# A hybrid decoder layer on one core: modulation sums moved to the u and c stages, FFN2's first group taken last, another prologue, narrower rotors

## The chip, the cores and the metric

The kernel runs on one core of a Trainium2 chip. The core has a matrix engine (TensorE, PE in the profile, with its weight loads as PEld), VectorE (DVE), ScalarE (ACT), GpSimd (POOL) and SyncE (SP), which issues nearly all DMA transfers here. Each engine works through its own instructions in program order; semaphores make one wait for another. The metric is the device time of one execution in microseconds, as the median of several. A second kernel differs from the first by the diff further down, and the question is how its time stands to the first one's.

## What is computed

One decoder layer over 1024 tokens of width 1024, all in f32: a half-step SwiGLU feed-forward net (FFN1, inner width 2816), a mixer of a gated convolution and a diagonal state-space model side by side, a second SwiGLU net (FFN2), and a final norm. Each sub-layer's input is RMS-normalised and modulated by a shift and a scale, and its output by a gate; these nine vectors are `silu(cond) @ w_mod + b_mod`.

```python
c_act = silu(cond)
sh1, sc1, g1, sh2, sc2, g2, sh3, sc3, g3 = split(c_act @ w_mod + b_mod, 9)
h = modulate(rms_norm(x, ffn1_norm), sh1, sc1)
x = x + 0.5 * g1 * swiglu(h, ffn1_w_gate, ffn1_w_up, ffn1_w_down)
h = modulate(rms_norm(x, mix_norm), sh2, sc2)
b, c, v, u = split(h @ w_in, 4)                       # 512 columns each
y_conv = b * conv3_causal(c * v)
y_ssm = glu(gelu(s5(u)))                              # 32 groups x 64 complex states
x = x + g2 * (concat(rms_norm(y_conv), rms_norm(y_ssm)) @ w_out)
h = modulate(rms_norm(x, ffn2_norm), sh3, sc3)
x = x + 0.5 * g3 * swiglu(h, ffn2_w_gate, ffn2_w_up, ffn2_w_down)
return rms_norm(x, final_norm)
```

## The kernel before

Activations lie transposed: x is eight tiles of 128 channels by two token halves (h = 0 and 1) of 512 columns. Every f32 product is made of three matmuls (`mm3`, L333): weights and activations are each split into a rounded high part and a low part (hi·hi, hi·lo, lo·hi). A weight tile therefore costs ACT one copy and DVE one subtraction (`w<-raw` in the profile), an activation tile the same (`split_act`, L346).

**Weights.** `Weights` (L114) holds the order of all weight arrays (1 MB each, called raw, two buffers) and of the *granules* made of them (1024 columns, split, called w). A granule is made when a slot of the ring comes free (`free`, `pump`), a raw is loaded when an earlier one has given its last granule (`ahead`).

**Clock.** The program is written out by Python. `mm3` ticks a `Clock` (L59) once for its three matmuls. Work put on it with `after(ticks, fn)` is emitted that many ticks later; every `period` ticks one step of a *side* generator is emitted. So the clock sets where, in each engine's order, side work stands among the matmuls. In the prologue the order is the written one (`InOrder.strict`).

**Stages.** PE goes through p (FFN1's group 0, the only one whose products start while the inputs land), fa1 to fa10 (the other ten groups of 256 inner columns; from fa4 on a seven-product scheme, `seven`, L575, replaces eight block products), fad and fald (the down product: eight groups in seven-product form, `down7`, and groups 0, 9 and 10 plainly), u, c and v, the states, b, glu (gl), w_out (wo), then FFN2: fb0, fb1 to fb10, fbd, and fb10d as the last plain part. Results of a group that its down product needs later are stored to DRAM (`keep`, L482; tensors keptN) and fetched back (`fetch`).

**Prologue** (L735 to L824). SP issues the load of tile 0's modulation weights (mw), x, the first raw, mw 1, mw 2, the second raw, then the other mw. `mods_of(k)` (L762) makes tile k's scale and shift: two sums of 128x1024 on DVE and two small operations. Then come the sums of squares, `roots` (an inverse square root in some 13 small DVE operations) and, tile by tile, the normalised and modulated activations. For tiles 0 and 1 there are two weights, w[0] and w[1], for the first two products; the other two are made after tile 1, and their products for tiles 0 to 2 come with tile 2's.

**Modulation sums.** The other seven vectors are 56 sums of one 128x1024 weight tile (wm) with the activated condition (cact): `mod_vector` (L452), one DVE instruction and a read each, in the order of `later`: G1, SC2, SH2, G2, SC3, SH3, G3, eight sums each. `mod_tile` sums one and issues the load of a next one on SP, so loads run a few sums ahead. G1 comes among fa's products; SC2, SH2, G2 in the second half of the down product (`side2`, L1132, period 8, L1209); SC3, SH3, G3 while glu and w_out run (L1414 onwards, period 8, then none, then 3), with cact fetched back from DRAM (cact_d). In the down product the wm tiles lie in the 20 buffers of activations (movA).

**State-space set-up** (`ssm_base`, `ssm_batch` L1031): side work among fa1 to fa10. For eight batches of four groups it makes matrices for the later state recursion and stores them. `rotors(i, op)` (L1069) makes the cosine (co) and sine (si) rotation tables from a base table (16 entries, rt) and a step table (8 entries, rs): two products and a sum, of 128x512 each. The two halves of the 128 partitions carry the same angles, for the sine with opposite signs.

**u, c, v and the states.** `u` is made for token half 0 (four weights at once), then half 1, weight by weight; after each, `across` (L1268) stores a tile to u_d in eight small transfers. Behind the last, `state_loads` loads a batch back in another layout (ub). `states(b)` (L1337) and `outputs(b)` (L1362) are put on the clock at 20 + 16b and 42 + 16b ticks: px (PE) from ub, X (ACT), an exchange of halves by DMA (swx), three DVE operations, a scan of four, si and co (DVE), another exchange (swz), co again, then yy (PE) and a gelu. Both exchanges use one buffer (sw). `outputs(b)` also issues the loads of later batches. Between them PE runs c and v, whose products DVE multiplies (cs), and the convolution (ya) runs on DVE.

**glu and w_out.** The two branch norms nA and nB are on the clock: sums (nBast), roots on DVE, a wide copy (nBarb), a spread by PE (nBabc).

**FFN2.** `group0` (L1503) makes group 0's inner activations, fb_0a and fb_1a; `down2` (L700) multiplies them by their down weights within fb1, between fb1's first and second granule, 96 matmuls and 16 updates `x<-fb0d,gate,x`. `combos` makes meanwhile the block sums (S1 to S4) that `seven` needs. The last part (L1568 on) takes groups 9 and 10 only: for each of eight output tiles d, token half 0 in 512 columns, half 1 partly in two pieces of 256, twelve matmuls per tile; `after2` (L1548) collects the final norm's squares, and the first sums come 6 ticks after d = 7, the spread another 11 ticks later.

Of the kernel before, what the change touches and what calls it, by code (L numbers as in the profile page):

```python
# [21 lines left out]
P = 128  # L22
# [16 lines left out]
LAST = ((0, NGRP - 2, NGRP - 1), (NGRP - 2, NGRP - 1))  # L39
# [77 lines left out]
class Weights:  # L117
# [7 lines left out]

    def __init__(self, engines, srcs, granules, raw_bufs):
# [9 lines left out]
        self.sums_pool = None  # L136
        self.slots = deque()
# [22 lines left out]
    def combine(self, j):  # L160
# [5 lines left out]
        self.sums[j] = {"t1": r[1], "t2": r[0], "t3": f, "t4": r[0]}  # L166

    def split_done(self, j, c):

        if j in self.combined and c in (0, "t2"):  # L170
# [61 lines left out]
def hymba_layer(ctx: ExitStack, tc, x_d, wm1_d, wmod_d, gu1_d, gs1_d, ds1_d, wl1_d, win_d, wout_d, glu_d, gu2_d, gs2_d, wd2_d, ds2_d, wl2_d, cols_d, cond_d, lam_d, bc_d, out_d):  # L232
# [54 lines left out]
    def stream(gu, gs, wd, ds, wl, m):  # L287


        for g in range(m):  # L290
            plain([gu[2 * g], gu[2 * g + 1]])
        for g in range(m, NGRP):
            j = len(srcs)
            inner = g == 1
            srcs.extend([gs[g - m, 0], wd, gs[g - m, 1]] if inner else [gs[g - m, 0], gs[g - m, 1]])
            seven = [(i, c) for i in (j, j + 1 + inner) for c in Weights.SEVEN]
            seven = [seven[i : i + 2] for i in range(0, 14, 2)]
            if inner:
                granules.extend(seven[:1] + [[(j + 1, 2 * q), (j + 1, 2 * q + 1)] for q in range(2)] + seven[1:])
            else:  # L300
                granules.extend(seven)
# [5 lines left out]
        plain([wl[i] for i in range(wl.shape[0])])  # L307

    stream(gu1_d, gs1_d, None, ds1_d, wl1_d, SEVEN_FROM[0])
    plain([win_d[i] for i in range(8)] + [glu_d] + [wout_d[i] for i in range(4)])  # L310
    stream(gu2_d, gs2_d, wd2_d, ds2_d, wl2_d, SEVEN_FROM[1])
    ws = Weights((V, A, SP, nc.gpsimd), srcs, granules, 2)
    ws.raw_pool = lambda i: rawp
# [162 lines left out]
    def gu_evac(fi, h, pg, pu, a_tiles, name):  # L476
        sg, af = t2k(f"{name}sg"), t2k(f"{name}af")
        A.activation(sg[:], pg[:], AF.Silu)
        V.tensor_tensor(out=af[:], in0=sg[:], in1=pu[:], op=ALU.mult)
        a_tiles[fi, h] = split_act(af[:], name + "a")  # L480

# [37 lines left out]

    def down(h, wd, groups, n, name, after):  # L520

        for d0 in range(0, KT, 4):
            outs = [ps(f"{name}d{d}_{h}") for d in range(d0, d0 + 4)]
            for q, a_tiles in enumerate(groups):
                for fi in range(2):
                    for i, o in enumerate(outs):
                        mm3(o[:], wd[2 * q + d0 // 4], 4 * fi + i, a_tiles[fi, h], q == fi == 0, q == len(groups) - 1 and fi == 1)
            for i, o in enumerate(outs):
                d = d0 + i
                V.scalar_tensor_tensor(out=x[d][h], in0=o[:], scalar=gate[:, n, d : d + 1], in1=x[d][h], op0=ALU.mult, op1=ALU.add)  # L530
                if after is not None:
                    after(d, h)
# [42 lines left out]
    def seven(name, between, place=1, kept=None, then=None):  # L575
# [4 lines left out]
        for side in "gu":  # L580
# [17 lines left out]
            for n, (left, b) in enumerate(SEVEN):  # L598
# [45 lines left out]
                if side == "g" and n == place:  # L644
                    between()
                if side == "u" and then is not None:
                    then(left)
        return a_tiles

# [50 lines left out]
    def down2(a_tiles, n, name, halves=(1, 0)):  # L700
        wd = ws.take(2)
        for dh in range(2):
            for h in halves:
# [957 lines left out]
```

## Time and profile before

| | |
|---|---|
| median of three runs | 1749.49 us (1746.47 to 1751.61) |
| the profiled execution's own time | 1752.1 us |
| its span, first to last instruction | 1750.3 us |
| granted TensorE clock, mean over the span | 0.989 |
| share of the span in the chain that ended last | PE 76%, DVE 14%, DMA 5%, issue 2% |
| HBM traffic over the span | 171 GB/s |
| DVE, weight splits w<-raw | 295.9 us in 358 operations |
| DVE, modulation sums wm | 76.6 us in 56 operations |

In a row of instruction groups stand the source line, engine, operation, output <- inputs by the program's names, then minimum, median and maximum duration in ns, or busy us and mean ns. Nearly all instructions have line 107, since a helper records them; tile names tell the stages apart. A row of a timeline begins with its start in us and the time it covers, and ends with its count and, in brackets, the idle time ahead of it and what ended that. A row of waits ends with total us, times and the longest. A busy PE is not PE at full clock: the granted clock is shown by window.

### The profile page before, as it was taken

To read this page: it belongs to the slowest core of one execution; us is meant where nothing else is said; L and a number is where in the kernel's file an instruction comes from. 1 tells how busy PE (TensorE), PEld (TensorE's weight loads), DVE (VectorE), ACT (ScalarE), POOL (GpSimd) and SP (SyncE) were. 2 spreads that over 40 slices of the span, in tenths; PEclk is the share of its full clock that TensorE was granted. 3 is DMA by queue.
4 is the path that set the end of the run, shared out by engine and by line. 5 is a ranking of instruction groups with operands and counts; after the bars stand their busy time and mean duration, and the time that the engine had idled before them with its cause. 6 is when DMAs were issued, how large, how long until landed. Compare 5 with 4: busy or idle time off the path is not lost.

```text
span 1750.3 us, 20808 instructions
## 1 busy us (share of the span) xinstructions
PE 1677.9 (96%) x7532; PEld 1379.6 (79%) x7532; DVE 1300.6 (74%) x2286; ACT 566.0 (32%) x934; POOL 351.1 (20%) x241
## 2 busy tenths in 40 slices
PE   4999999999999999999999899989999999999996
PEld 3788887878787888887877778778888888888886
DVE  7999999999855687744656977967777666676656
ACT  4223234444322221332113424423343443322221
POOL 0000132222222221100000022023323322333211
PEclk9999999999999999999999999999999999999998
DMA  8245544444597877134654450113444334669312
GB/s 319 85 145 196 207 167 165 182 169 178 196 391 266 326 256 292 56 84 149 210 157 140 144 191 25 48 46 135 157 162 173 147 133 156 239 242 366 115 49 96
DMA packets 101080, 304.54 MB, mean 174 GB/s; under 512 B 19057, under 2 KB 34673, under 8 KB 89842
## 3 DMA queue, kind: packets, MB, share of 16 engines
q1 hardware_dynamic: 100978, 303.22, 48.4%
q8 instruction: 59, 0.97, 0.2%
q14 instruction: 43, 0.35, 0.1%
HBM read 212.47 MB, written 86.51 MB: 171 GB/s over the span
## 4 chain that ended last, share of the span: by engine, by line
PE 76%; DVE 14%; DMA 5%; issue 2%; POOL 1%; ACT 1%; SPq 1%; DVEq 0%; POOLq 0%; ACTq 0%
PE wo L107 4%; PE fald L107 3%; DVE w L107 3%; PE p L107 2%; PE fb10d L107 2%; PE fbd_0B L107 2%; PE fbd_1B L107 2%; PE u L107 2%; DMA swz<-si 2%; PE b L107 1%; DVE x L107 1%; PE c L107 1%; PE fa3u L107 1%; PE fb0g L107 1%; PE fa2g L107 1%
## 5 line engine op out<-in xcount | busy, mean ns | idle before, releaser
L107 ACT CAST w<-raw 128x512 fp32r<-128x512 f32 (+1 forms) x358 | 236.2, 689 | 484.3 <-issue 75.0
L107 DVE TENSOR_TENSOR w<-raw,w 128x512 fp32r<-128x512 f32 (+1 forms) x358 | 295.9, 845 | 107.3 <-ACT w L107 106.5
L164 POOL TENSOR_TENSOR sums<-raw 128x512 f32<-128x512 f32 x50 | 71.4, 1429 | 451.5 <-DMA raw<-in_gs 263.3
L173 POOL TENSOR_TENSOR raw<-sums,raw 128x512 f32<-128x512 f32 x50 | 77.7, 1554 | 371.1 <-DVE w L107 358.9
L175 POOL TENSOR_TENSOR raw<-raw 128x512 f32<-128x512 f32 x50 | 77.5, 1549 | 89.6 <-DVE w L107 73.0
L107 DVE CUSTOM_DVE_ANT_0 wm<-wm,cact 128x1024 f32<-128x1024 f32 x56 | 76.6, 1375 | 16.9 <-DMA wm<-in_wmod 16.9
L165 POOL TENSOR_TENSOR raw<-raw 128x512 f32<-128x512 f32 x50 | 77.3, 1547 | 3.2
L366 POOL TENSOR_TENSOR n3aq<-n3aq,n3aq 128x512 f32<-128x512 f32 x5 | 8.3, 1666 | 281.4 <-DMA wm<-in_wmod 255.7
L107 PE MATMUL p<-h,w 128*128 128x512 f32 x192 | 50.0, 423 | 8.0 <-DVE h L107 5.1
L107 DVE TENSOR_TENSOR w<-sums,w 128x512 fp32r<-128x512 f32 x50 | 52.5, 1063 | 3.6 <-ACT w L107 3.0
L107 PEld LDWEIGHTS p<-h,w 128*128 128x128 f32 x192 | 39.4, 207 | 18.4 <-DVE h L107 6.4
L107 PE MATMUL v<-h,w 128*128 128x512 f32 x192 | 46.9, 395 | 0.0
L107 PE MATMUL c<-h,w 128*128 128x512 f32 x192 | 46.6, 395 | 0.0
L107 PE MATMUL wo<-oa,w 128*128 128x512 f32 x192 | 45.6, 392 | 0.9 <-DVE w L107 0.7
L107 PE MATMUL b<-h,w 128*128 128x512 f32 x192 | 45.6, 394 | 0.0
L107 PE MATMUL wo<-ob,w 128*128 128x512 f32 x192 | 45.5, 392 | 0.0
L107 PE MATMUL u<-h,w 128*128 128x512 f32 x192 | 44.7, 392 | 0.2 <-DVE h L107 0.2
L107 PEld LDWEIGHTS wo<-oa,w 128*128 128x128 f32 x192 | 35.8, 188 | 9.0 <-DVE w L107 1.1
L107 PEld LDWEIGHTS u<-h,w 128*128 128x128 f32 x192 | 35.7, 188 | 8.2 <-DVE h L107 0.6
L107 PEld LDWEIGHTS wo<-ob,w 128*128 128x128 f32 x192 | 35.8, 188 | 7.7 <-DVE ob L107 0.4
L107 PEld LDWEIGHTS b<-h,w 128*128 128x128 f32 x192 | 35.6, 188 | 7.1
L107 PEld LDWEIGHTS c<-h,w 128*128 128x128 f32 x192 | 35.4, 188 | 7.0
(1565 smaller groups left out, 4056.2 us busy)
## 6 DMA issues: line engine op xcount, KB each, us to landing
raw<-in_gs SPq DMA_DIRECT2D x34, 1024.0 KB, 5.5
wm<-in_wmod SPq DMA_DIRECT2D x56, 512.0 KB, 5.3
raw<-in_ds SPq DMA_DIRECT2D x16, 1024.0 KB, 7.2
raw<-in_gu SPq DMA_DIRECT2D x10, 1024.0 KB, 7.0
mw<-in_wm SPq DMA_DIRECT2D x8, 1024.0 KB, 12.8
x<-in_x SPq DMA_DIRECT2D x16, 512.0 KB, 8.0
raw<-in_win SPq DMA_DIRECT2D x8, 1024.0 KB, 5.4
raw<-in_wl SPq DMA_DIRECT2D x5, 1024.0 KB, 6.7
```

Of the source, the lines that this page charges most:

```text
L107: r = getattr(self.engine, name)(*args, **kw)
L164: self.G.tensor_tensor(out=f, in0=r[2], in1=r[1], op=ALU.subtract)
L165: self.G.tensor_tensor(out=r[1], in0=r[1], in1=r[0], op=ALU.subtract)
L173: self.G.tensor_tensor(out=r, in0=s["t3"], in1=r, op=ALU.add)
L175: self.G.tensor_tensor(out=r, in0=self.chunk(j, 3), in1=r, op=ALU.subtract)
L366: nc.gpsimd.tensor_tensor(out=a, in0=a, in1=sq[:, :n], op=ALU.add)
```

## The change

Five edits:

1. *Prologue.* mw 1 is loaded before the first raw, and both raws before mw 2; `mods_of(1)` comes before the roots. Tiles 0 and 1 are normalised and modulated together; the other two weights are made right after, and products of all four weights run for both tiles, then four for each further tile.
2. *Rotors.* Base and step tables are kept in a packed form with two groups on each half of the partitions, so that the three operations are 128x256. Each half's result is stored to both halves in DRAM, for the sine with one negated copy by ACT.
3. *x.* The last x loads of FFN1's down product are issued after its third left operand (A22), not its second.
4. *Modulation sums.* G2 leaves the down product. G2, SC3, SH3 and G3 (32 sums) start with u's second token half, at period 3; what is left is emitted before b. glu and w_out have none; cact stays in SBUF.
5. *FFN2's group 0.* Its activations are kept in DRAM like group 9's; `down2` is gone; the last part of the down product has groups 0, 9 and 10. fb1 is made by a new function, `seven_early`, with its own order of the seven products, gate and up side together; a fourth ring slot is opened for the last part.

```diff
-LAST = ((0, NGRP - 2, NGRP - 1), (NGRP - 2, NGRP - 1))
+LAST = ((0, NGRP - 2, NGRP - 1), (0, NGRP - 2, NGRP - 1))
...
+    EARLY = (0, 3, "t4", "t1", "t2", "t3", 2)
...
+            if g == 1:
+                two = j, j + 1
+                granules.extend([(j, c), (j + 1, c)] for c in Weights.EARLY)
             else:
-                granules.extend(seven)
+                seven = [(i, c) for i in (j, j + 1) for c in Weights.SEVEN]
+                granules.extend(seven[i : i + 2] for i in range(0, 14, 2))
...
+    EARLY = (("A11", "A"), ("A12", "A"), ("A22", "E"), ("S1", "C"), ("S2", "B"), ("S3", "D"), ("S4", "C"))
+
+    def seven_early(name, kept):
...
+        for left, b in EARLY:
+            (w,) = ws.take()
+            for q, side in enumerate("gu"):
...
+                for k in range(4):
+                    while len(blocks[left]) <= k:
+                        clock.step()
+                    mm3(bank[b][:], w, 4 * q + k, blocks[left][k], opens and k == 0, k == 3, more=not opens)
...
+            ws.free()
...
     mod_load(0)
     load_x(range(2))
-    ws.load(1)
-    for k in range(1, KT):
+    mod_load(1)
+    ws.load(2)
+    for k in range(2, KT):
         mod_load(k)
-        if k == 2:
-            ws.load(2)
...
+    mods_of(1)
     y = roots(st, 8, D, "p")
...
+    for k, h in ((0, 0), (1, 0), (0, 1)):
+        scaled(k, h)
+    shifted(0)
+    scaled(1, 1)
+    shifted(1)
+    for k in range(2):
         for h in range(2):
...
+            part(h, k, (0, 1))
+    ws.open(ringp, 1)
+    ws.open(ring1, 1)
+    w4 += ws.take(2)
+    for k in range(2):
         for h in range(2):
...
+            part(h, k, (2, 3))
+    for k in range(2, KT):
+        mods_of(k)
+        for h in range(2):
+            scaled(k, h)
+        shifted(k)
         if k < KT - 1:
-            for h in range(2):
-                part(h, k, (0, 1))
-            for j in range(0 if k == 2 else k, k + 1) if k > 1 else ():
+            for outs in ((0, 1), (2, 3)):
                 for h in range(2):
-                    part(h, j, (2, 3))
+                    part(h, k, outs)
...
-    cact_d = scratch.tile([P, 1024], F32, name="cact_d")
-    SP.dma_start(cact_d[:], cact[:])
...
-            return a[:, :512].rearrange("p (g m i) -> p g m i", g=GB, m=8)
+            return a[:, :256].rearrange("p (g m i) -> p g m i", g=2, m=8)
...
-            V.tensor_tensor(out=r[:, :512], in0=r[:, :512], in1=t[:, :512], op=op)
-            SP.dma_start((co_d, si_d)[i][b], r[:, :512])
+            V.tensor_tensor(out=r[:, :256], in0=r[:, :256], in1=t[:, :256], op=op)
+            if i:
+                A.activation(r[:, 256:512], r[:, :256], AF.Identity, scale=-1.0)
+            for q, half in enumerate(halves):
+                to = slice(256 * q, 256 * q + 256)
+                if i == 0:
+                    SP.dma_start(
+                        co_d[b].rearrange("(d p) f -> p d f", d=2)[:, :, to], r[half, :256].unsqueeze(1).to_broadcast([64, 2, 256])
+                    )
+                else:
+                    SP.dma_start(si_d[b][half, to], r[half, :256])
+                    SP.dma_start(si_d[b][halves[1 - q], to], r[half, 256:512])
...
-    down7("fad0", lefts[0], 0, lambda left: fetch_chunk(1, left), lambda left: load_x(range(2), (1, 3)) if left == "A12" else None)
+    down7("fad0", lefts[0], 0, lambda left: fetch_chunk(1, left), lambda left: load_x(range(2), (1, 3)) if left == "A22" else None)
     clock.period = 8
-    clock.side.append(side2(mod_mov, (SC2, SH2, G2)))
+    clock.side.append(side2(mod_mov, (SC2, SH2)))
...
             ready(act2, h, KT)
+            clock.period = 3
+            clock.side.append(side2(mod_mov, (G2, SC3, SH3, G3)))
             for i in range(4):
...
+    while clock.side:
+        clock.step()
     wb = ws.take(4)
...
-    clock.period = 8
-    clock.side.append(side2(lambda name: wmp.tile([P, 1024], F32, tag="wm", name=name, bufs=2)[:], (SC3, SH3, G3)))
...
-    seven("fb1", lambda: down2(a_prev, 2, "fb0", (0, 1)), 0, kept[1])
+    seven_early("fb1", kept[1])
...
+    ws.sums_pool = None
+    first_open.close()
+    sums_open.close()
+    ring1 = ctx.enter_context(tc.tile_pool(name="ring1c", bufs=1))
+    ws.open(ring1, 1)
...
+    def last_part(dh, h, tok, tiles, free=False):
+        outs = {d: ps(f"fb10d{d}_{h}_{tok.start}") for d in tiles}
+        for q, (w, a) in enumerate(zip(wd, (*a_last, a_prev))):
+            for fi in range(2):
+                for d, o in outs.items():
+                    mm3(o[:, tok], w, 4 * fi + d % 4, a[fi, h], q == fi == 0, q == 2 and fi == 1, tok)
...
     for dh in range(2):
-        wd = ws.take(2)
+        wd = ws.take(3)
         for h in range(2):
             for tok in PIECES[h] if dh else WHOLE:
...
+                ds = range(4 * dh, 4 * dh + 4)
+                if h and not dh:
+                    last_part(dh, h, tok, ds, True)
+                else:
+                    for d in ds:
+                        last_part(dh, h, tok, [d])
+    ws.free(3)
```

More of the change, by code (lines that the diff above doesn't have):

```diff
@@ L136, in __init__ @@
         self.sums_pool = None
+        self.early = ()
         self.slots = deque()
@@ L518, in proj @@
         return o
[L520 to L532, printed above, removed]
     blocks = {}
@@ L573, in hymba_layer, with seven @@
     SECOND = (("A11", "A"), ("S2", "B"), ("A12", "A"), ("S3", "B"), ("S1", "C"), ("A22", "B"), ("S4", "C"))
-    def seven(name, between, place=1, kept=None, then=None):
+    def seven(name, kept=None, then=None):
         a_tiles, gate_, taken = {}, {}, []
@@ L1016, in ssm_base @@
                 n *= 2
-        for i in range(2):
-            A.copy(baset[i][:], base[i][:].rearrange("p i g -> p g i"))
+        for tab, to in zip((base, step), packed):
+            for i in range(2):
+                for half, part in enumerate((lo, hi)):
+                    A.copy(
+                        to[i][part].rearrange("p (b q) n -> p n b q", q=2),
+                        tab[i][part].rearrange("p n (b s q) -> p n b s q", s=2, q=2)[:, :, :, half, :],
+                    )
         yield
@@ L1473, in hymba_layer @@
     w_out((0, 1), 1, 1)
-    clock.period = 3
     ws.free(2)
```

191 lines of the change are left out of this document (102 added, 89 removed).

## The prediction

> **What bounds the kernel now.** I read the page's span and busy times first, then the busy time by windows, TensorE's waits, and the timelines of the stages that the change touches.
>
> ```profile
> span 1750.3 us, 20808 instructions
> PE 1677.9 (96%) x7532; PEld 1379.6 (79%) x7532; DVE 1300.6 (74%) x2286; ACT 566.0 (32%) x934; POOL 351.1 (20%) x241
> ```
>
> TensorE (PE) bounds: it idles 1750.3 − 1677.9 = 72 us, and the change drops no product. A gain can come only from that idle time and from half-clock stretches behind stalls. The windows (length; busy time of PE, its weight loads, VectorE (DVE), ScalarE (ACT), GpSimd (POOL); granted clock) show where those lie:
>
> ```profile
> 200.00:300.00 100.00, 97.90 (x443) 80.22 (x442) 93.36 (x147) 37.77 (x67) 28.18 (x20) 1.00 0.44 158
> 300.00:400.00 100.00, 97.43 (x438) 79.22 (x437) 94.32 (x150) 40.14 (x72) 28.65 (x18) 0.98 0.49 180
> 500.00:600.00 100.00, 96.14 (x405) 77.61 (x404) 62.41 (x80) 24.50 (x44) 30.21 (x21) 0.97 0.85 327
> 750.00:800.00 50.00, 49.93 (x226) 41.22 (x225) 19.10 (x33) 15.72 (x23) 0.00 (x0) 1.00 0.36 95
> 800.00:850.00 50.00, 46.98 (x243) 39.05 (x243) 28.50 (x47) 9.54 (x13) 0.00 (x0) 1.00 0.56 167
> 950.00:1000.00 50.00, 42.41 (x188) 34.66 (x188) 42.61 (x95) 19.55 (x30) 0.00 (x0) 0.93 0.40 130
> 1150.00:1200.00 50.00, 50.00 (x213) 40.99 (x214) 34.55 (x51) 18.20 (x32) 12.31 (x9) 0.97 0.27 102
> 1200.00:1650.00 450.00, 450.00 (x1987) 372.85 (x1986) 305.41 (x427) 159.93 (x282) 142.88 (x97) 1.00 0.50 185
> ```
>
> The 1200–1650 row is the pace: 450/1987 = 0.2265 us for a 512-column matmul, with nothing left to gain there. PE's waits (total, times, longest) name the stalls:
>
> ```profile
> PE yy L107 <- DVE co L107: 5.2, 6, 1.3
> PE fb0d L107 <- DVE x L107: 5.1, 4, 2.0
> PE p L107 <- DVE h L107: 5.1, 2, 2.6
> PE nBabc L107 <- DVE nBarb L107: 3.9, 1, 3.9
> PE fad_0A L107 <- DVE w L107: 2.8, 2, 1.7
> PE p L107 <- ACT h L107: 2.8, 2, 1.6
> PE fa7gC L107 <- DVE fa7gt L107: 2.6, 1, 2.6
> PE fa5uC L107 <- DVE fa5ut L107: 2.1, 1, 2.1
> PE gl L107 <- DVE yg L107: 1.9, 1, 1.9
> PE fad_0B L107 <- ACT w L107: 1.8, 1, 1.8
> PE nAbbc L107 <- DVE nAbrb L107: 1.7, 1, 1.7
> ```
>
> **Prologue: −8.** Stage p (FFN1's group 0):
>
> ```profile
> L107 PE MATMUL p<-h,w x192: 387/390/797, 30.5 to 86.8; 128*128 128x512 f32 x192
> 46.41 7.92 PE L107 MATMUL p<-h,w 128*128 128x512 f32 x22 [2.57 <-DVE h L107]
> 45.20:52.00 6.80, 5.59 (x13) 4.45 (x14) 6.80 (x16) 1.39 (x2) 0.00 (x0) 0.50 0.79 304
> ```
>
> It lasts about 56.5 us for 192 × 0.2265 = 43.5, so 13 are lost: 7.9 in the four waits, the rest at half clock, 3.4 of it in the 45.2–52 row. The change loads tile 1's modulation weights ahead of the FFN weights and sums them before the roots (about 0.6 later for the first matmul), prepares tiles 0 and 1 together and lets all four weights work on them: 48 matmuls (10.9 us) while DVE makes the next tiles. The waits at 43–46 and their half clock go (4.1 + 3.4), and some of the first tile's 4.1 with them; 0.6 comes back: −8, bounds −6 and −9.5. Cover: DVE's next tile must cost no more than PE's 24 matmuls on it (5.4 us); by rows quoted below it is two sums of 1.22 and four operations of 0.75, 5.4 with nothing overlapped, so DVE just keeps up.
>
> **Rotors: −4.** 48 DVE operations go from 512 to 256 columns.
>
> ```profile
> L107 DVE TENSOR_TENSOR rot<-rot,rott 128x512 f32<-128x512 f32 x16 | 16.0, 1001 | 0.2
> L107 DVE TENSOR_TENSOR rott<-rs,rt 128x512 f32<-128x512 f32 x16 | 15.3, 959 | 2.1 <-DMA co_d<-rot 2.1
> L107 DVE TENSOR_TENSOR rot<-rs,rt 128x512 f32<-128x512 f32 x16 | 14.2, 885 | 0.1
> L107 DVE SCALAR_TENSOR_TENSOR x<-fb10d,gate,x x20: 477/750/752, 1689.1 to 1735.4; 128x512 f32<-128x512 f32 x12, 128x256 f32<-128x256 f32 x8
> ```
>
> They cost 45.5 us between 169 and 454. The last row has both widths: 477 against 750 ns, 0.64 of it; so 16 to 23 us of DVE are saved. It pays only where PE waits for DVE: fa5 2.1, fa7 2.6 and a half-clock stretch (0.02 × 100 = 2). Eight small ACT negations and 32 more DMA issues on SP lie where ACT is at 38 to 40%; an issue costs SP 0.35 (the raw row further down). Bounds 0 (the same stall moves to the next DVE burst) and −8; −4 is the middle.
>
> **x loads later: −2.** The last x half of token 1 goes behind SP's two raw loads for the down product:
>
> ```profile
> 532.35 0.54 SPq L107 DMA_DIRECT2D x<-in_x  x1
> 532.98 1.28 SPq L107 DMA_DIRECT2D raw<-in_ds  x2
> ```
>
> The weights that fad_0A and fad_0B wait for (4.6) hang on these loads; half a megabyte less ahead of them is 1.6 us at the 327 GB/s of the 500–600 row, plus a share of its 3 us of clock. Bounds 0 and −5.
>
> **Modulation sums: −10 and +25.** Each reads 512 KB and costs DVE 1.2 us:
>
> ```profile
> L107 DVE CUSTOM_DVE_ANT_0 wm<-wm,cact x56: 1207/1223/2310, 157.7 to 1048.2; 128x1024 f32<-128x1024 f32 x56
> ```
>
> In glu and w_out none is left. There they stood before and inside the scalar chains that nAbbc and nBabc wait for: 3.9 + 1.9 + 1.7 of waits, 3.5 of clock (0.07 × 50). I take −10, bounds −6 and −11.
>
> In u and c 32 of them come, one per three ticks (2.0 us of PE): DVE has 31 us idle in the 750–800 row, 21 in 800–850, so by busy time they fit. The order does not. Their buffers rotate over four, and SP issues in order. Sum 12's load (counted from 1, of G2, SC3, SH3, G3) waits for sum 8, which DVE has behind the product cs·v_0, and that needs v_0, done as px starts, at 799.8. Behind loads 12 and 13 on SP stand a weight load, the eight u_d stores of the last u tile and the ub load that px needs. Before:
>
> ```profile
> 786.52 0.35 SPq L107 DMA_DIRECT2D raw<-in_win  x1
> 786.92 5.83 SPq L107 DMA_DIRECT2D u_d<-ya  x8
> 792.79 0.91 SPq L107 DMA_DIRECT2D ub<-u_d  x2
> DMA to landing us min/median/max: 3.3/3.9/4.4
> 799.82 1.05 PE L107 MATMUL px<-ub,mi 128*128 128x128 f32 x8
> 817.08 0.69 DVE L107 TENSOR_TENSOR co<-co,swz 128x512 f32<-128x512 f32 x1 [2.43 <-DMA swz<-si]
> ```
>
> From raw to ub's landing (the row of 3.3 is ub's) that took 6.3 + 3.3 = 9.6 us. Now: v_0 done 799.8, cs·v_0 0.7, sums 8 and 9 2.4 → load 13 issues at 803.2, raw at 803.7, ub lands at 813.3. PE stands 13.5 us in front of px 0, with v_0's second half queued behind it, and then runs 3.4 us at half clock: +1.7. Bounds 10 and 18 (the 2 MB ahead of the stores).
>
> What is late next: swx_0 on SP stands behind loads 18 and 19, which wait for sums 14 and 15, loaded only after ub; X_0 on DVE stands behind sums 17 to 19 and v_0's second half. So co_0, 17.3 us behind px 0 before (817.08 − 799.82), comes at some 26, and PE has about 24 us of work up to yy 0: +2. px 2 now stands three matmuls behind yy 0, which releases its ub load (3.9 to land): +4.5 and +1.7 of clock. yy 1 has 12 matmuls ahead and a chain of 13 us: +2. yy 2 has two sums in its chain: +1.6. Together 13.5 + 1.7 + 2 + 6.2 + 2 + 1.6 = 27, plus some 5 of the later yy waits, less the 7 that 750–900 loses now (5.2 of yy and small px waits): +25, bounds +5 (ub not held) and +38.
>
> **Group 0 of FFN2 last: −9 and −2.5.** The second product of group 0 leaves fb1 and joins the last part:
>
> ```profile
> 1124.28 1.43 PE L107 MATMUL fb0d<-fb_0a,w 128*128 128x512 f32 x5
> 1155.82 2.89 PE L107 MATMUL fb1gC<-h3S,w 128*128 128x512 f32 x12
> 1736.94 0.71 PE L107 MATMUL n_0bc<-ident,n_0rb 128*128 128x128 f32 x4 [2.52 <-DVE n_0rb L107]
> ```
>
> 31.5 us for 96 matmuls (21.7): 9.8 lost, waiting for 16 DVE updates of x. The 96 come back at full pace (72 of 512 and 48 of 256 columns). Cover in the new fb1: S1's blocks are ready near 1127 and 1130, PE wants them at 1138; both raw buffers are held until the last granule is split, at 1145, so fb2's first weight comes at 1155, wanted at 1160. Four stores and four fetches of 512 KB lie in windows at half DMA load. −9, bounds −4 (a stall of 5 at fb2) and −10. The 1150–1200 row grants 0.97, 1.5 us of clock behind waits of 1.9 to 2.0, and this is part of the 9.8. [...]
>
> In the last part each d has six ticks, not four, so the first quarter's normalisation (17 ticks after its d 7) falls before the last matmul (24 ticks), not behind it (16): its 2.5 us stall at 1736.9 leaves the tail. Bounds 0 and −4.
>
> **Sum.** −8 − 4 − 2 − 10 + 25 − 9 − 2.5 = −10.5. The profiled execution took 1752.1 (1.8 outside its span), 2.6 above the median 1749.5 of three; so 1741.6 for such an execution and 1739 for the median.
>
> **Rivals.** (a) SP does not hold ub: sum 8 runs ahead of v_0's end and the state chain keeps its rhythm. For it: 31 idle us of DVE before 800. Against it: the order above. The +25 falls to about +3: 1749.5 − 32 = 1717. (b) Slower, by the SP queue between px 0 and yy 5: each exchange load stands behind modulation loads that wait for DVE, and each of six states' chains gets 5 us longer instead of the 1.6 to 4.5 above: 13.5 + 1.7 + 6 × 5 + 5 − 7 = +43, so 1749.5 − 35.5 + 43 = 1757. For it: the chains are already what yy waits for. It decides from a stage cost of 36 up. (c) The early gains do not arrive: DVE, at 93 to 94% in 200–400, is as late for fa as before, so the prologue's 8 and the rotors' 4 are lost behind it: 1739 + 12 = 1751, no change. For it: PE is then 8 us ahead of a DVE that is not.
>
> **How the numbers follow.** Forecast 0.56, (a) 0.12, (b) 0.18, (c) 0.14. About 0.3% (5 us) is what a measurement of this kernel can tell from no change. The forecast's own range, 1730 to 1748, lies faster for 0.5 of its 0.56; with (a) and a bit of (c) 0.66. Same: 0.15; slower: 0.19, nearly all (b). The range takes (a)'s value and part of (b): 1717 to 1757.
>
> **What would show it.** After's p stage ending near 79; no fb0d group and no wait at fb1gC; no nBabc wait; above all PE idle some 13 us in front of the first px, released by ub's DMA, and waits at the first yy's; the last matmul to the end 2.5 shorter. Wrong if px 0 follows v_0 at once (a), if waits between 800 and 920 exceed 36 (b), or if fa5, fa7 or earlier groups wait as much as p gained (c).

## The result, and the profile after

The changed kernel takes 1762.8 us, the median of three runs (1761.0 to 1764.0), against 1749.5: ratio 1.0077, 95% interval 1.0049 to 1.0104. It is slower, outside the predicted range and on the other side of no change. Its profiled execution has a span of 1759.3 us, 9.0 above the other's (that one lay 2.6 above its median, this one 1.8 below), and all stage lengths below come from these two. First the page's span and busy times, then TensorE's waits over the whole span:

```profile
span 1759.3 us, 20928 instructions
...
PE 1675.5 (95%) x7556; PEld 1381.4 (79%) x7556; DVE 1274.1 (72%) x2270; ACT 569.6 (32%) x948; POOL 349.8 (20%) x241
```

```profile
PE px L107 <- DMA ub<-u_d: 27.9, 6, 17.0
...
PE fa4gC L107 <- DVE fa4gt L107: 4.5, 1, 4.5
PE fb1gA L107 <- ACT fb1gt L107: 4.1, 1, 4.1
...
PE n_256bc L107 <- DVE n_256rb L107: 3.0, 1, 3.0
...
PE fa7gC L107 <- DVE fa7gt L107: 2.3, 1, 2.3
PE px L107 <- issue: 1.8, 1, 1.8
PE yy L107 <- DVE co L107: 1.6, 2, 1.2
...
PE fb1gC L107 <- DVE fb1gt L107: 1.3, 1, 1.3
```

PE's busy time is 2.4 lower and its idle time 11.4 higher. The waits that the change was to remove are gone (fb0d, nBabc and nAbbc have no row any more), and the list is now headed by one that was 0.6 us before: the load of ub, 27.9. Two new ones stand beside it, at fa4gC and fb1gA. The windows, with the columns of before:

```profile
45.20:52.00 6.80, 6.80 (x31) 5.63 (x30) 6.54 (x13) 2.24 (x4) 0.00 (x0) 1.00 0.90 349
200.00:300.00 100.00, 95.48 (x421) 77.98 (x420) 94.53 (x156) 38.87 (x71) 25.62 (x17) 0.97 0.51 173
750.00:800.00 50.00, 39.06 (x173) 32.03 (x171) 25.02 (x38) 11.28 (x17) 0.00 (x0) 0.93 0.57 169
800.00:850.00 50.00, 36.23 (x166) 30.50 (x167) 34.80 (x62) 6.82 (x9) 0.00 (x0) 0.83 0.84 269
950.00:1000.00 50.00, 48.89 (x237) 40.32 (x236) 40.16 (x88) 25.93 (x41) 0.00 (x0) 1.00 0.22 68
1100.00:1150.00 50.00, 45.89 (x192) 37.43 (x191) 49.57 (x71) 23.19 (x39) 17.81 (x6) 0.93 0.17 64
1200.00:1650.00 450.00, 450.00 (x1987) 372.78 (x1986) 306.57 (x428) 159.25 (x281) 138.68 (x94) 1.00 0.50 186
```

The last row is that of before to the microsecond: nothing happened where PE was the only limit. The row 45.2–52 is now full and at full clock. The row 200–300 is worse than before (4.5 idle, 0.97), with DVE as busy as it was (95%, before 93%). The rows 750–850 lost 24.7 us of PE where 3.1 were lost, at a clock of 0.93 and 0.83.

Set against the prediction's terms, by the start of each stage's first matmul in the two timelines (us):

| stretch | before, us | after, us | difference | predicted |
|---|---|---|---|---|
| start to the first fa1 | 87.0 | 76.5 | −10.5 | −8 |
| fa1 to the first fad | 418.2 | 421.7 | +3.5 | −4 |
| fad to the first fald | 162.6 | 159.6 | −3.0 | −2 |
| fald and u, to the first c | 115.7 | 114.8 | −0.9 | 0 |
| c to the first glu | 162.5 | 195.6 | +33.1 | +25 |
| glu to the first fb0 | 130.2 | 119.3 | −10.9 | −10 |
| fb0 to the first fb2, of before less the 21.7 us of moved matmuls | 93.3 | 92.1 | −1.2 | −9 |
| fb2 to the end, of before with these 21.7 | 580.8 | 579.7 | −1.1 | −2.5 |
| sum | | | +9.0 | −10.5 |

Three terms make up the miss: u and c (8 worse), fb1 (8 worse), and FFN1's first groups, which gave back what p gained (5 worse than the −12 of both). SyncE's queue in the largest of them:

```profile
781.80 10.83 SPq L107 DMA_DIRECT2D wm<-in_wmod  x3
792.72 0.38 SPq L107 DMA_DIRECT2D raw<-in_win  x1
793.16 9.52 SPq L107 DMA_DIRECT2D u_d<-ya  x8
802.72 0.91 SPq L107 DMA_DIRECT2D ub<-u_d  x2
803.72 9.02 SPq L107 DMA_DIRECT2D wm<-in_wmod  x6
```

Three modulation loads take 10.8 us to issue because they wait for buffers, and raw, the u_d stores and ub stand behind them, as foreseen. But the eight stores themselves now take 9.5 us, not 5.8. Most of the difference is waiting: by the waits of SP's queue, SP stands among them 2.7 us until the raw ahead has landed and 1.8 until a modulation load has, where before it was 1.9 for the raw alone. And TensorE there:

```profile
806.08 2.05 PE L107 MATMUL px<-ub,mi 128*128 128x128 f32 x8 [17.02 <-DMA ub<-u_d]
807.78 6.67 PE L107 MATMUL v<-h,w 128*128 128x512 f32 x24
...
834.49 0.39 PE L107 MATMUL yy<-co,mo 128*128 128x127 f32 x2
834.63 0.95 PE L107 MATMUL v<-h,w 128*128 128x512 f32 x3
841.47 2.08 PE L107 MATMUL px<-ub,mi 128*128 128x128 f32 x8 [5.89 <-DMA ub<-u_d]
```

px 0 waits 17.0, then px and v run at half clock at first (granted 0.50 from 806 to 809 and 0.62 to 810; 2.05 for eight px, 1.05 before; 6.67 for 24 v matmuls, 5.4 at full pace). px 2 stands three matmuls behind yy 0 and waits 5.9 for its own ub, which is loaded only once yy 0 has read the buffer. In all, PE idles 32.3 us from c to glu against 5.7, and its busy time there is 163.3 us against 156.8 for the same products: 26.6 of the 33.1 are waits and 6.5 are half clock.

### The profile page after: what moved, and what is told of

Read it like the earlier page. It is cut to its first block, busy times and chain, and to the rows that moved or that the text cites. A ratio compares the mean times of both kernels' runs of the same rounds, so it can differ in the third digit from the quotient of the medians.

```text
span 1759.3 us, 20928 instructions
## 1 busy us (share of the span) xinstructions
PE 1675.5 (95%) x7556; PEld 1381.4 (79%) x7556; DVE 1274.1 (72%) x2270; ACT 569.6 (32%) x948; POOL 349.8 (20%) x241
## 4 chain that ended last, share of the span: by engine, by line
PE 68%; DVE 12%; DMA 6%; issue 2%; SPq 1%; POOL 1%; ACT 1%; DVEq 0%; POOLq 0%; ACTq 0%
PE wo L107 5%; PE fb10d L107 4%; PE fald L107 3%; DVE w L107 2%; PE b L107 2%; PE u L107 2%; PE fbd_1B L107 2%; PE fbd_0B L107 2%; PE fad_1B L107 2%; DMA wm<-in_wmod 2%; PE c L107 1%; PE fad_0B L107 1%; PE fbd_1C L107 1%; PE fbd_0C L107 1%; PE fbd_1A L107 1%
## 5 line engine op out<-in xcount | busy, mean ns | idle before, releaser
L167 POOL TENSOR_TENSOR sums<-raw 128x512 f32<-128x512 f32 x50 | 78.2, 1563 | 469.6 <-DMA raw<-in_gs 289.6
L183 POOL TENSOR_TENSOR raw<-sums,raw 128x512 f32<-128x512 f32 x48 | 73.7, 1535 | 333.8 <-DVE w L107 307.3
L185 POOL TENSOR_TENSOR raw<-raw 128x512 f32<-128x512 f32 x48 | 72.9, 1518 | 71.0 <-DVE w L107 71.0
L107 DVE CUSTOM_DVE_ANT_0 wm<-wm,cact 128x1024 f32<-128x1024 f32 x56 | 68.8, 1238 | 23.7 <-DMA wm<-in_wmod 23.5
L168 POOL TENSOR_TENSOR raw<-raw 128x512 f32<-128x512 f32 x50 | 75.8, 1516 | 3.2
L107 PE MATMUL p<-h,w 128*128 128x512 f32 x192 | 46.0, 402 | 1.3 <-ACT h L107 1.3
L107 PE MATMUL wo<-ob,w 128*128 128x512 f32 x192 | 45.2, 391 | 0.0
L107 PEld LDWEIGHTS v<-h,w 128*128 128x128 f32 x192 | 37.1, 199 | 7.4
```

Source lines behind the costliest of these rows:

```text
L107: r = getattr(self.engine, name)(*args, **kw)
L167: self.G.tensor_tensor(out=f, in0=r[2], in1=r[1], op=ALU.subtract)
L168: self.G.tensor_tensor(out=r[1], in0=r[1], in1=r[0], op=ALU.subtract)
```

## The experiments

Stage lengths are from each kernel's own profile. Kernels with a single run (no interval) are judged by their stage, since totals scatter (13 runs of the kernel before: 1746.2 to 1751.9 us). Stages scatter too: where kernels have the same code, one stage can differ by 2 to 4 us, as shown below.

**The sums at their old places.** All other edits stay.

```diff
-    clock.side.append(side2(mod_mov, (SC2, SH2)))
+    clock.side.append(side2(mod_mov, (SC2, SH2, G2)))
...
-            clock.period = 3
-            clock.side.append(side2(mod_mov, (G2, SC3, SH3, G3)))
...
+    clock.period = 8
+    clock.side.append(side2(lambda name: wmp.tile([P, 1024], F32, tag="wm", name=name, bufs=2)[:], (SC3, SH3, G3)))
...
+    clock.period = 1000
...
+    clock.period = 3
...
+    while clock.side:
+        clock.step()
```

> The changed kernel with its modulation sums put back where they were: G2 in the second half of FFN1's down product, SC3, SH3 and G3 while glu and w_out run (cact stays in SBUF). Theory, that the move of the sums loses 33 us between the first matmul of c and the first of glu and gains 11 from there to fb0: c to glu back to 162 to 165 us (195.7 in the changed kernel), glu to fb0 back to about 130, the total 22 us below the changed kernel, about 1741, so 8 to 9 below the one before. Rival, that c to glu is longer for another reason (other weight loads, the prologue's or FFN's new order shifting DMA traffic): c to glu stays above 180 and the total above 1750.

Measured: 1740.8 us, ratio to the kernel before 0.9943 (0.9928 to 0.9958). c to glu 161.7 us, glu to fb0 127.4. Its windows:

```profile
750.00:800.00 50.00, 50.00 (x226) 41.52 (x226) 16.63 (x22) 15.26 (x23) 0.00 (x0) 1.00 0.38 105
800.00:850.00 50.00, 47.38 (x245) 39.09 (x243) 32.02 (x54) 11.57 (x16) 0.00 (x0) 1.00 0.59 185
```

So the moved sums cost more than the 13 us that the change lost: 22 us between the medians of the two changed kernels. By stages that is 34 in c to glu, less 8 gained up to fb0; and FFN1 took some 5 longer in this profile than in the other, 3 of them before the down product, where the code is the same. The other four edits together (with cact kept in SBUF) make a kernel that is 0.6% faster than before.

**The loads on another queue.** Is it SP's order, or the traffic?

```diff
-            SP.dma_start(r, wmod_d[n - 2, b, :, i, :])
+            (nc.gpsimd if n in (G2, SC3, SH3, G3) else SP).dma_start(r, wmod_d[n - 2, b, :, i, :])
```

> The changed kernel with only the loads of the 32 sums in u and c issued from GpSimd's queue, which has no other work there, instead of SP's; the same sums in the same places on VectorE. Theory, that px 0 waits because the u_d stores and the ub load stand behind held loads on SP: the wait before the first px falls from 17.2 us to under 3 and its half clock goes, c to glu falls from 195.7 to about 170 (the sums on VectorE inside the state chain remain), the total to about 1738. Rival, that 32 sums are too much work or traffic for this stage (24 us of VectorE, 16 MB): the same waits come up at other px and yy, c to glu stays above 185 and the total above 1752.

Measured: 1758.6 us (ten runs, 1751.0 to 1762.6), ratio 1.0044 (1.0028 to 1.0060). c to glu is still 190.5. TensorE's waits from 780 to 960, and DVE's timeline ahead of the first state:

```profile
PE yy L107 <- DVE co L107: 21.1, 5, 18.5
PE px L107 <- DMA ub<-u_d: 7.6, 2, 7.2
```

```profile
821.46 1.23 DVE L107 CUSTOM_DVE_ANT_0 wm<-wm,cact 128x1024 f32<-128x1024 f32 x1 [1.44 <-DMA wm<-in_wmod]
...
822.69 1.23 DVE L107 CUSTOM_DVE_ANT_0 wm<-wm,cact 128x1024 f32<-128x1024 f32 x1
...
824.27 0.69 DVE L107 TENSOR_TENSOR X<-co,X 128x512 f32<-128x512 f32 x1
```

The theory failed, and the rival's numbers came. Without modulation loads on SP px 0 waits 7.2, so about 10 of the 17 were SP's order. The eight u_d stores take 9.2 us here too (SP waits among them 2.9 us for the raw to land and 2.8 for earlier stores), so the rest goes with the loads under way beside them, whose traffic delays what SP waits for, not with SP's order. But in this kernel the order on DVE came out with all 32 sums ahead of X of state 0, most of them waiting for their loads (the DMA engines were busy 99% of 768.3 to 783.9), and yy 0 waits 18.5 in px 0's place. So the traffic counts, as the rival had it, and the order decides whom it holds: the hold moved from one in-order engine to the next.

**The sums from c on.** SP is past the ub loads when they start.

```diff
-            clock.period = 3
-            clock.side.append(side2(mod_mov, (G2, SC3, SH3, G3)))
...
+    clock.period = 3
+    clock.side.append(side2(mod_mov, (G2, SC3, SH3, G3)))
```

> The changed kernel with the 32 sums started behind the issue of the first state loads, at the first matmul of c, instead of in u's second half. Theory (order on SP): no wait of more than 2 us before the first px, 17 + 3.4 of the loss gone, but the loads now stand among the later exchanges for all 32 sums: waits at px 1 to 7 and yy of 12 to 20 us in all, c to glu about 178 to 185. Rival (work and traffic of the stage): c to glu within 5 us of 195.7.

Measured: 1751.8 us (one run), c to glu 180.5. As expected, there is no wait at px 0, but:

```profile
PE px L107 <- DMA ub<-u_d: 15.9, 5, 6.2
```

The longest is at px 2 again. c to glu is 18 us longer than before without any hold of px 0, so half of the 33 isn't that hold. In the built order of PE's matmuls, yy 0 has 20 matmuls between itself and px 2 in the kernel before and with the sums put back; with sums among the states it has 3. The order of each engine is settled when the program is built; in these builds, where sums stand in the chain in front of yy 0, yy 0 has moved back until it stands right before px 2, whose load can then hide behind nothing. That the longer chain is why the order came out so is inferred from these orders, not tested.

**Fewer sums there.** G2 in u, the other 24 from c on:

```diff
-            clock.side.append(side2(mod_mov, (G2, SC3, SH3, G3)))
+            clock.side.append(side2(mod_mov, (G2,)))
...
+    clock.side.append(side2(mod_mov, (SC3, SH3, G3)))
```

> The changed kernel with G2's eight sums left in u's second half and the other 24 started behind the issue of the first state loads. So far c to glu lasts 162 us with no sum in it, 180.5 with all 32 from c on, 195.7 as the change has it. Theory, that two things add: loads held in front of the u_d stores (the 17 us wait at the first px and its half clock, only where load 12 is issued ahead of them) and some 0.6 us for each sum that stands among the states: here no wait over 2 us at the first px and 162 + 24 x 0.6 = 176 (174 to 178). Rival, that traffic in u already delays the stores (eight loads of 512 KB): a wait of 5 or more at the first px, c to glu above 180.

Measured: 1754.4 us (one run), c to glu 183.4 where a fixed price per sum would have given 176. Its waits:

```profile
PE px L107 <- DMA ub<-u_d: 14.1, 4, 6.6
PE px L107 <- DMA mi<-mi_d: 3.3, 1, 3.3
```

px 0 doesn't wait, so eight sums in u hold nothing. But there is no fixed price of a sum: the modulation loads on SP delay the states' own loads (ub, and now mi), and px 2 stands right behind yy 0 here too, with no matmul between them.

**13 sums in u, faster, and the other 11 after glu's norms** (on the kernel with the sums put back):

```diff
+            clock.period = 2
...
+            clock.side.append(side_u(13))
...
-    clock.side.append(side2(lambda name: wmp.tile([P, 1024], F32, tag="wm", name=name, bufs=2)[:], (SC3, SH3, G3)))
...
+    clock.side.append(side3())
```

> The kernel of mods_back with 13 sums (SC3 and the first five of SH3) in u's second half at period 2, so that every load ahead of the u_d stores waits only for a sum that VectorE has ahead of the product with v_0, and the last 11 behind both norms of glu, in a fixed order. Theory, that not the traffic but a load held for v_0 made the wait at the first px: that wait is under 3 us, c to glu 162 to 166; glu to fb0 119 to 122; total 1732 to 1737. Rival, traffic: 6.5 MB of loads within u's second half delay the u_d stores by 4 or more, seen at the first px; total 1739 or above.

Measured: 1743.1 us, ratio 0.9964 (0.9951 to 0.9976); px 0 waits 6.7, c to glu 169.9, glu to fb0 125.2. The last of the 13 ran at 793, ahead of the states, none stands in a state's chain, and px 0 still waits, so the theory's result didn't come. But the run doesn't decide for traffic alone, since loads were still held: SP waited 3.5 us between 775 and 780 for the buffers of three of them, whose sums stand behind a weight split on DVE. Beside that the 16 stores ahead of the last eight took 15.0 us to issue, against 10.2 with the sums put back: SP waited 6.8 us among them for loads to land, not 1.8.

**SC3 in u, SH3 and G3 after the norms, DVE's order fixed:**

```diff
+            clock.side.append(side2(mod_mov, (SC3,)))
...
+    def side3():
+        while fetched:
+            InOrder.strict = True
+            mod_tile(wm_home if later else None)
+            InOrder.strict = False
+            yield
```

> The kernel of mods_back with the sums placed by what the runs so far show: G2 in the down product, only SC3 (8 sums) in u's second half, none in c, v and the state chain, SH3 and G3 (16) behind both norms of glu, in w_out, in an order fixed on VectorE. Theory: c to glu stays at 162 (no load is held in front of the u_d stores), glu to fb0 falls from 127.5 to 119 to 122 because no sum stands in the chain of nAb and nBa; total 1733 to 1737. Rival, that eight loads in u already delay the u_d stores, or that two buffers are too few in w_out: a wait of 3 or more at the first px, or waits of wo for its weights; total at or above 1741.

Measured: 1744.9 us (one run); c to glu 161.4, but glu to fb0 133.1, with 4.6 us of wait at the third norm's sums. VectorE waits 15.1 us for wm loads from 1000 to 1080: two buffers of wm are probably too few for sums packed so late, as the rival had it.

**SC3 in u, SH3 and G3 where they were:**

```diff
+            clock.period = 3
+            clock.side.append(side2(mod_mov, (SC3,)))
...
-... (SC3, SH3, G3)))
+... (SH3, G3)))
```

> The kernel of mods_back with SC3's eight sums in u's second half at period 3 and the other 16 where before had them (from b on, none early in w_out, period 3 late). Theory: c to glu stays at 161 to 163; glu to fb0 falls from 127.5 only in part, because a few sums still stand in the chains of nAb and nBa: 121 to 126; total 1735 to 1740. Rival, that the sums in glu cost the same whether 16 or 24 are left: total 1741.

Measured: 1735.8 us, ratio 0.9924 (0.9907 to 0.9941), which beats both kernels. c to glu 160.6, glu to fb0 127.7. Eight sums in u cost nothing, but the eight fewer between glu and fb0 bring nothing there either (127.4 with all 24), where 121 to 126 was expected. Its 5 us over the kernel with the sums put back are spread over several stages, and the two intervals overlap, so the step from one to the other isn't settled.

**The prologue, the rotors, and both put back** (on the kernel with the sums put back). The diffs are those of edits 1 and 2, reversed.

> The kernel of mods_back (the change without its move of the sums) with the prologue of before put back as well. The new prologue ended stage p 10.5 us earlier, but fa4 then waits 5.2 us for VectorE (and 3 at half clock), which before did not. Theory, that VectorE limits p to fa4 and takes most of that gain back: with the old prologue p ends 10.5 later, the wait at fa4's C product goes, and the end of fa10 is only 2 to 4 us later; total 1743 to 1745. Rival, that the wait at fa4 comes from the rotors' new tables or order, not from the prologue: it stays, the end of fa10 and the total are 10 later, about 1751.

> The kernel of mods_back with the rotors of before (48 operations of 512 columns, 16 stores) put back. Theory, that the narrower rotors take load off VectorE where PE waits for it: the waits at fa4, fa5, fa7 and fa9 grow together by 4 to 10 us and the end of fa10 is that much later, total 1745 to 1751. Rival, that the rotors are hidden (VectorE's other bursts set the waits): the end of fa10 within 2 us of mods_back's 501.7, total within 2 of 1741.

> The kernel of mods_back with both the prologue and the rotors of before, so that of the change only the last group, the x loads and cact in SBUF are left. Each put back alone moved the end of fa10 by less than 2 us (502.1 and 500.5 against 501.7). Theory, that both relieve the same slack of VectorE between p and fa5 and each alone takes it up: with both back the end of fa10 is 3 to 5 us later than with either (504 to 506, as before's 505.4), total 1743 to 1746. Rival, that neither matters: the end of fa10 stays at 500 to 502.5 and the total at 1739 to 1741, and before's 505.4 had another reason.

Measured, one run each: 1739.4, 1741.1 and 1746.4 us. fa10 ends at 502.1 us with the old prologue, 500.5 with the old rotors, 503.8 with both old, and between 497.5 and 501.7 in the eleven kernels that have both edits. From 503.8 that makes 3 for the new prologue alone, 2 for the new rotors alone and 2 to 6 for both, though the old prologue ends p 9 us later (85.7 for 76.7). The eleven, with the same code up to there, lie 4 us apart, so none of these gains is settled to better than that; but in all of these comparisons less than 5 of p's 9 us reach fa10. The waits of PE from 200 to 500, old prologue first, then old rotors:

```profile
PE fa7gC L107 <- DVE fa7gt L107: 3.8, 1, 3.8
```

```profile
PE fa4uC L107 <- DVE fa4ut L107: 4.1, 1, 4.1
PE fa7gC L107 <- DVE fa7gt L107: 2.6, 1, 2.6
PE fa4gC L107 <- DVE fa4gt L107: 1.9, 1, 1.9
```

With the old prologue there is no wait at fa4; with the new one PE comes to fa4 earlier and waits there for DVE. Against the kernel before, in the kernel after DVE's addition fa4gt came at 230.4 us against 233.9, 3.5 earlier, where p ended 10.5 earlier.

**fb1's weight freed later, by program text and by a forced order:**

```diff
+                    if side == "u":
+                        InOrder.strict = True
+                        ws.free()
+                        InOrder.strict = False
-            ws.free()
```

(The first run is the same without the two strict lines, on the kernel after; the second is on the kernel with the sums put back.)

> The changed kernel with one ring slot given back later: group 0's last weight slot is freed after fb1's first product has been copied out of its bank, so that on ScalarE the two copies of that product stand ahead of the weight copy that waits for GpSimd's sums. Theory, that the 4.1 us wait before fb1's second product is ScalarE's queue held by that weight copy: the wait and its half clock go, fb0 to the end of fb1 falls from 92.2 by 3 to 7 us, less what S1's blocks are then late. Rival, that the product waits for its weights (the sums on GpSimd take 9.4 us beside VectorE): the wait stays, at the next product, and the stage changes by less than 2.

> The kernel of mods_back with ScalarE's order in fb1 fixed by hand: the weight copies of the third product (which wait for GpSimd) stand behind the copies of the first product, as the late free alone did not bring about. Theory, that PE's 4.1 us wait ahead of fb1's second product is ScalarE's queue held by these copies: the wait and its half clock go, some of it comes back as a wait for S1's blocks; first matmul of fb0 to first of fb2 falls from 92.7 by 3 to 7 us. Rival, that GpSimd's sums (one of 9.4 us beside VectorE) are what fb1 waits for in any order: the same 4 to 7 us stand at the third product instead, the stage changes by less than 2.

Measured: 1764.8 and 1738.0 us (one run each). The text alone left the order on ACT as it was, and fb1gA's wait at 4.1. The forced order halved it to 2.0, and fb1gC then waited 3.1; fb0 to fb2 is 92.4 and 93.1 (92.1 in the kernel after, 92.7 with the sums put back). ACT's order isn't what costs.

**fb1's block sums on VectorE** (on the kernel with SC3 in u). GpSimd in the kernel after, then DVE and ACT at the same place:

```profile
1123.04 9.44 POOL L167 TENSOR_TENSOR sums<-raw 128x512 f32<-128x512 f32 x1 [23.14 <-DMA raw<-in_gs]
1132.56 1.63 POOL L168 TENSOR_TENSOR raw<-raw 128x512 f32<-128x512 f32 x1
1134.15 3.42 POOL L176 TENSOR_TENSOR raw<-sums,raw 128x512 f32<-128x512 f32 x2
1137.55 3.38 POOL L178 TENSOR_TENSOR raw<-raw 128x512 f32<-128x512 f32 x2
```

```profile
1131.25 0.68 DVE L107 TENSOR_TENSOR fb<-fb,fb0u 128x512 f32<-128x512 f32 x1
1131.85 1.18 DVE L107 TENSOR_TENSOR f<-f,f 128x512 f32<-128x512 f32 x1
1132.96 3.47 DVE L107 TENSOR_TENSOR f<-h 128x512 f32<-128x512 f32 x2
```

```profile
1139.29 0.62 ACT L107 CAST w<-raw 128x512 fp32r<-128x512 f32 x1 [4.56 <-POOL raw L178]
...
1141.98 0.58 ACT L107 COPY fb1gt<-fb1gA 128x512 f32<-128x512 f32 x1
```

GpSimd's first sum is recorded at 9.4 us (spans on POOL are rough, but its next operation and ACT's wait begin accordingly), beside a row of VectorE operations without a gap. When it ends, VectorE's own operations take 1.7 instead of 0.68 while GpSimd makes its other five. ACT waits for the last two of these with the copy that PE needs queued behind. By these rows the two engines held each other up: 9.4 us for the one, where a sum of the same shape took 1.29 at 1097.3, and 1.7 for 0.68 for the other. By what means isn't shown.

```diff
-        self.G.tensor_tensor(out=f, in0=r[2], in1=r[1], op=ALU.subtract)
-        self.G.tensor_tensor(out=r[1], in0=r[1], in1=r[0], op=ALU.subtract)
+        E = self.V if j in self.early else self.G
+        E.tensor_tensor(out=f, in0=r[2], in1=r[1], op=ALU.subtract)
+        E.tensor_tensor(out=r[1], in0=r[1], in1=r[0], op=ALU.subtract)
```

(and so in `split_done`, for the same two raws.)

> As m_sc3_in_u (modulation sums: SC3 in u, SH3 and G3 after glu's norms; all other edits as after), but the six block sums of fb1's two raws (sums and raw, 128x512) are made on VectorE, not on GpSimd. Theory (what fb1 waits for is the GpSimd operation that lasts 9.4 us beside an unbroken row of VectorE additions, and VectorE's own slower additions beside GpSimd): the six take 0.7 us each on VectorE, the stretch of 1.7 us additions goes, PE's waits at fb1gA (4.1) and fb1gC (1.7) fall below 2 in sum, and fb0 to fb2, 91.8 us in m_sc3_in_u, becomes 86 to 89; span 1729 to 1732. Rival (VectorE is simply full in fb0 and fb1, whoever makes the sums): the six operations add 4.2 us to it, the waits stay at 5 to 8 us, fb0 to fb2 stays 91 to 95, span 1733 to 1738.

Measured: 1737.1 us, ratio 0.9929 (0.9907 to 0.9952), fb0 to fb2 89.8 us against 91.7 (91.6 to 92.7 in all kernels that make fb1 as the change does). The total is not below that kernel's 1735.8. PE's waits there, and a window behind them:

```profile
PE fb1uC L107 <- DVE fb1ut L107: 2.3, 1, 2.3
PE fb1gC L107 <- ACT fb L107: 0.8, 1, 0.8
PE fb1gD L107 <- DVE fb1gu L107: 0.8, 1, 0.8
```

```profile
1150.00:1157.00 7.00, 4.71 (x14) 3.81 (x15) 7.00 (x10) 2.48 (x5) 4.37 (x3) 0.76 0.00 0
```

The wait at fb1gA is gone, so GpSimd's late sums made it. But a wait for DVE comes at the last product, with half clock behind it (twelve matmuls in 4.48 us, 2.88 at full pace), and only 2 of the 3 to 6 us arrive. The rival's reason, a full VectorE, isn't what the trace shows there: ahead of the addition fb1ut that PE waits for (1151.6 us), VectorE had stood 2.6 us for fb1gD and 1.8 for ACT's copy of a weight whose subtraction comes first in its order. What holds this last wait was not tested.

## Why the prediction was wrong

*Sums in u and c: +25, measured +33.* The mechanism was right: SP holds ub, PE stands in front of px 0, then px 2 waits behind yy 0. The waits from 780 to 970 came to 32.3 (27.9, 1.8, 1.6 and 1.0), below the 36 from which rival (b) was to decide. The step that failed is the size of three terms. First, "v_0 done 799.8 … ub lands at 813.3" took raw to ub's landing as 9.6 us from the row of before; it took 13.4 (792.7 to 806.1), because the eight stores alone took 9.5, with SP waiting among them for the raw and a modulation load to land. That gave 17.0 for 13.5, inside the bounds of 10 and 18 that were written down, but at their end: 3.5 of the 8. Second, half clock stood in the sum with 1.7 and 1.7, each for 3.4 us at half clock, which is what before's trace shows behind its wait at 1149.9 (granted 0.56, 0.50, 0.50 and 0.73 in the four us from 1151). PE's busy time in the stage grew by 6.5: 3.1 more, since half clock lasted 3.7 us behind px 0 (from 806.1), 5.8 behind px 2 (from 841.5), and came behind px 3 too, for 3.4 (from 861.0). Third, the other waits grew by some 1.5 more than in the sum, and not where it had them: the yy waits, which were to grow, fell from 5.2 to 1.6, and waits of px 1, px 3 and px 4 took their place.

*glu and w_out: −10, measured −10.9.* Right. nAbbc and nBabc have no wait, and the window 950–1000 is at full clock.

*Prologue −8 and rotors −4: measured −10.5 in p, then +3.5 in fa1 to fa10.* The step that failed is the one that added the two and booked p's gain as the kernel's. Where the prologue was costed, its cover was looked for within p ("DVE just keeps up"), and it was there. That PE would then be ahead of a DVE busy at 93 to 94% stood in rival (c), at 0.14, and is what the runs with one edit put back show: of the 9 us in p, fa10 keeps 3 beside the old rotors (503.8 to 500.5) and 0.4 to 4.6 beside the new ones (502.1 to between 501.7 and 497.5). In the kernel after, −7 of −12 was left. The sum should have treated the two edits as one gain of VectorE's, which at fa10 is 2 to 6 us against both put back.

*x later: −2.* fad came out 3.0 shorter. No run took this edit alone, and in the 14 kernels that have it this stretch lasts 159.6 to 162.2 us, against 162.6 in the one profile of before. So how much of it is the edit's isn't shown.

*Group 0 out of fb1: −9, measured −1.2.* "31.5 us for 96 matmuls … 9.8 lost" was read as a cost of those matmuls, and this cost did go. A new one came in its place:

```profile
1142.61 5.36 PE L107 MATMUL fb1gA<-h,w 128*128 128x512 f32 x12 [4.11 <-ACT fb1gt L107]
```

4.1 of wait, 2.5 of half clock (5.36 for 2.88) and 1.3 at fb1gC are 7.9, the whole miss. The step that failed is the check of cover, which allowed for a stall of 5 at most: it looked at when blocks and raws are ready at before's pace, and left out that GpSimd's sums and DVE's additions slow each other (9.4 us for a sum of 1.29 elsewhere, then 1.7 for 0.68 for each addition), and that a copy PE needs stands behind them on ACT. The 96 matmuls had also been 21.7 us of PE work beside which DVE made the block sums: from fb0 to fb2 DVE was busy 94.5 of 115.0 us before and 83.1 of 92.1 after. m_fb1_order and m_fb1_dve show the wait moving and not leaving. That the missing cover is why is argued from these times; no run put the 96 matmuls back alone.

*Tail: −2.5, measured −1.1.* The n_0bc wait fell from 2.5 to 1.4 and n_256bc remains at 3.0; right in kind.

## What to carry to other kernels

A side task that fits into an engine's idle time by the sum may still not fit by the order: ask which in-order queue its loads stand in, and what is issued behind them. A time read from a quiet row isn't the time under the new load: here 9.6 us became 13.4. Work that is removed from the bounding engine, or done earlier on it, is worth only as much as the next engine is ahead; look for matmuls that serve as cover before counting their stall as gain. Two edits that both free or both need the same engine are costed together.

## What the runs showed of the hardware

A GpSimd sum of 1.29 us elsewhere (at 1097.3 in the kernel after) was recorded in fb1 at 9.2 to 9.4 us in five kernels: the one after, with the sums put back, with fb1's weight freed late, with the forced order, and with SC3 in u. In the first and the last of these it stands beside an unbroken row of VectorE operations, and VectorE's went from 0.68 to 1.7 each while GpSimd made its next five. Eight small stores took 3.7 us to issue with no bulk load just ahead of them (before, at 768.0 us), 5.6 to 5.9 behind one raw of 1 MB, 9.5 behind two modulation loads and a raw, and 9.2 where the modulation loads had been issued by another queue; by the waits of SP's queue most of what is above 3.7 is waiting for earlier transfers to land. And the granted clock fell behind short waits: behind one of 2.3 us (fb1uC above) the window of 7 us shows 0.76. The length of a wait alone didn't decide it: in the kernel before, the 12 matmuls behind a wait of 2.0 us (1141.3) took 3.02 us, and the 18 behind one of 1.9 (1149.9) took 6.04, where 18 at full pace take 4.3.
